# Four weight tiles at four different start addresses modulo 256, in a one-core decoder layer

## The chip, the cores and the metric

The kernel runs on one core of one Trainium2 chip. The metric is device time in microseconds of one launch. The kernel before takes 2124.78 us, the median of three runs that lie between 2121.08 and 2126.06 us.

## The reference

One decoder layer on 2048 tokens of width 1024, all in float32: gated linear attention (GLA) with 4 heads, then a gated feed-forward network with a short causal convolution, each followed by a residual and a layer norm, and each with a shift, a scale and a gate computed from a conditioning vector. Cut to what matters here:

```python
def gla_mixer(h, w_in, w_a2, b_a, norm_g, w_o):
    q, k, v, r, a_lr = jnp.split(h @ w_in, ...)          # 1024 -> 3088 columns
    log_a = jax.nn.log_sigmoid(a_lr @ w_a2 + b_a) / 16
    ...                                                  # chunks of 64 tokens, state of 128 x 256 a head
    return (rms_norm(o) * norm_g * jax.nn.silu(r)) @ w_o

def conv_ffn(h, w_up, conv_w, conv_b, w_down):
    u, g = jnp.split(h @ w_up, 2, axis=-1)               # 1024 -> 2 * 2816 columns
    u = causal_conv3(u, conv_w) + conv_b
    return (jax.nn.silu(u) * g) @ w_down

x = layer_norm(alpha * x + (1 + gate) * sublayer(x * (1 + scale) + shift), g, b)   # twice
```

## The kernel before, in words

**Split products.** TensorE multiplies in the float32r format. To keep float32 precision each operand is split into a rounded part h and a remainder l. `split` (L103) makes h by a ScalarE copy (L104) and l by a VectorE subtraction (L107). `mm3` (L109) then issues three matmuls for a product: h by h (L110), h by l (L111), l by h (L112). Nearly all of TensorE's work is in these three lines. Each matmul loads a stationary operand of 128 columns (the profile's PEld rows) and streams a moving operand of 512 columns past it (the PE rows).

**Weights.** A split weight stands in a tile of the pool `hlp`: 128 partitions by 2 by 1024 elements of 4 bytes, 8192 bytes a partition, h in the first half and l in the second. `hl_tile` (L94) hands these tiles out under three tags: "h0" and "h1" with one buffer each and "h2" with two, so there are four tiles. In the profile all four are called hl. Every slice of them that a matmul reads starts a multiple of 512 bytes from the tile's start. A tile is filled in one of three ways: by `split` from a raw tile; by a DMA of the saved split weight (`hl<-wh_d`, 1 MB); or by a DMA of a raw weight into the second half, which is then split in place (`hl<-wf_d` and `hl<-wfc_d`, 512 KB, the output projection).

**Where things lie.** Pools are laid out one behind the other: small tiles (`const`, `smp`), the four raw tiles, the four hl tiles, the five temporaries of tag "t2", and so on. The hl tiles start at bytes 26112, 34304, 42496 and 50688 of each partition. All four are multiples of 256. So are the starts of the tiles that hold the other operand: xc (split activations of the input and feed-forward products), xg (split activations of the query and output projections), h (called h3 in the code: the narrow split weight of the feed-forward network) and dhl (both operands of the down product). The tile "still", which is multiplied by itself at the start to warm TensorE up, starts at 64 modulo 256. The two U tiles start at 0 and 128 modulo 256.

**Stages.** From 0 to about 500 us: the modulation vectors and the input projections (hl stationary with xc moving, and the other way round for the values). From about 500 to 860 us: the query projection of the second token block, the heads of the attention, the output projection (xg stationary with hl moving) and the first layer norm; TensorE alternates between short runs of split matmuls and plain float32 matmuls of the heads. From about 860 to 1690 us: the up product of the feed-forward network in a fixed loop of 44 rounds (h0, h1 and h2 tiles stationary, xc moving). To the end: the down product, whose operands are called dhl and every third time hl.

**What sets the order.** The order of the work is written out by hand (`at_unit`, `quarter`, `tick`), with priorities for some evictions. DMAs are issued on SyncE's queue.

Of the kernel before, what the change touches and what calls it, by code (L numbers as in the profile page):

```python
# [8 lines left out]
F32 = mybir.dt.float32  # L9
F32R = mybir.dt.float32r  # L10
# [6 lines left out]
P = 128  # L17
# [21 lines left out]
def kernel(  # L39
# [27 lines left out]
    smp = ctx.enter_context(tc.tile_pool(name="smp", bufs=6))  # L67
    rawp = ctx.enter_context(tc.tile_pool(name="rawp", bufs=4))
    hlp = ctx.enter_context(tc.tile_pool(name="hlp", bufs=4))
# [5 lines left out]
    def order(later, earlier):  # L75
        tc.add_manual_dep(later.ins, earlier.ins.name,
                          mybir.DependencyInfo(mybir.DependencyClass.NoSync, mybir.DependencyReason.DATA),
                          reason="issue order")
# [4 lines left out]
    def psum(tag, bufs=1):  # L83
        return ps.tile([P, 512], F32, tag=tag, name="ps_" + tag, bufs=bufs)
# [4 lines left out]
    def z_tile(name="z"):  # L89
        return zp.tile([P, 1024], F32, tag="z", name=name)  # L90

    turn = [0]

    def hl_tile(tag=None):  # L94
        if tag is None:
            if turn[0] < 6:
                tag = ("h0", "h1", "h2", "h2", "h2", "h2")[turn[0]]
            else:
                tag = (("h2", "h2", "h0", "h1") if turn[0] < 32 else ("h2", "h0", "h2", "h1"))[(turn[0] + 2 * (turn[0] >= 48)) % 4]
            turn[0] += 1  # L100
        return hlp.tile([P, 2, 1024], F32R, tag=tag, name="hl", bufs=2 if tag == "h2" else 1)

    def split(h, l, src, lsrc=None):  # L103
        accs["copy"] = nc.scalar.copy(h, src)  # L104
# [78 lines left out]
    def rsqrt_eps(o, i):  # L183
        nc.gpsimd.tensor_scalar(o, i, EPS, None, op0=ALU.add)
        nc.gpsimd.tensor_tensor(o, o, mhalf[:, 0:o.shape[1]], op=ALU.pow)
# [268 lines left out]
    if True:  # L454
# [877 lines left out]
        def state(H, s):  # L1332
            po, old, h = H["po", s], H["S"][s], H["h"]
            new = S32[:, h] if s == 3 else ab.tile([P, DV], F32, tag="St", name="St", bufs=6)
            with tc.high_priority(offset=150):
                if old is None:
                    nc.vector.tensor_copy(new, po)
                else:
                    nc.vector.scalar_tensor_tensor(new, old, H["el"][:, 1, s:s + 1], po, op0=ALU.mult, op1=ALU.add)
            H["S"].append(new)  # L1340

        def head_c(H, g):
            h, v, Q = H["h"], H["v"], H["Q"]
            if g == 0:
                H["on"] = zp.tile([P, 4, DV], F32, tag="z", name="on")
                H["ss"] = smp.tile([P, 4], F32, tag="ss", name="ss")
            on = H["on"]
            po = psum("w", 4)
            at = H["at"][g]
            for i in range(2):  # L1350
                s = 2 * g + i
                pos_ = po[:, i * DV:i * DV + DV]
                st = H["S"][s]
                nc.tensor.matmul(pos_, at[:, i], v[s], start=True, stop=st is None)  # L1354
                if st is not None:
                    nc.tensor.matmul(pos_, Q[:, s, 0:128], st, start=False, stop=True)  # L1356
            if g == 0 and ("po", 3) in H:
                state(H, 3)
            with tc.high_priority(offset=150):
                nc.scalar.copy(on[:, 2 * g:2 * g + 2].rearrange("p s c -> p (s c)"), po)  # L1360
# [23 lines left out]
                store(g_d[H["tb"]][H["h"]].rearrange("p (s c) -> p s c", s=2), sr)  # L1384

        def normalise(z, after=None):
            st = smp.tile([P, 2, 6], F32, tag="bst", name="bst")
            for i in range(2):
                bn = nc.vector.bn_stats(st[:, i], z[:, i * 512:i * 512 + 512])
                if after is not None:  # L1390
                    order(bn, after)
            mv = smp.tile([P, 2], F32, tag="mv", name="mv")
            nc.vector.bn_aggr(mv, st)
            rs = smp.tile([P, 2], F32, tag="rs", name="rs")
            rsqrt_eps(rs[:, 0:1], mv[:, 1:2])
            nc.gpsimd.tensor_scalar(rs[:, 1:2], mv[:, 0:1], rs[:, 0:1], -1.0, op0=ALU.mult, op1=ALU.mult)
            nc.scalar.activation(z, z, AF.Identity, bias=rs[:, 1:2], scale=rs[:, 0:1])
# [184 lines left out]
        for m in range(16):  # L1582
            H = heads[m]
# [48 lines left out]
    if True:  # L1632
# [122 lines left out]
        for n in range(2 * NJ):  # L1755
# [5 lines left out]
            st = dict(j=j, hf=hf, W=W, X=X0 if hf == 0 else XN, refill=XN if n == NJ - 1 else None)  # L1761
# [130 lines left out]
    def ln2_last(p, b, t):  # L1892
        a, sm = acc.pop((p, b, t))
        st = sts.pop()
        nc.vector.bn_stats(st[:, 1], a[:, 512:1024])
        mv = smp.tile([P, 2], F32, tag="mv", name="mv")
        nc.vector.bn_aggr(mv, st)

        rs = smp.tile([P, 2], F32, tag="rs", name="rs")
        nc.scalar.activation(rs[:, 1:2], mv[:, 1:2], AF.Sqrt, bias=eps[:, 0:1])  # L1900
        ys = []
        for half in range(2):
            cs_ = slice(half * 512, half * 512 + 512)
            y = t2p.tile([P, 512], F32, tag="t2", name="y")
            i = nc.vector.scalar_tensor_tensor(y, a[:, cs_], mv[:, 0:1], rows[2][half], op0=ALU.subtract, op1=ALU.mult)
            if half == 0:
                order(nc.vector.reciprocal(rs[:, 0:1], rs[:, 1:2]), i)
            cut = (0, 256, 512) if t == 3 and half == 1 else (0, 512)
            for c0, c1 in zip(cut, cut[1:]):
                nc.vector.scalar_tensor_tensor(y[:, c0:c1], y[:, c0:c1], rs[:, 0:1], rows[3][half][:, c0:c1],  # L1910
                                               op0=ALU.mult, op1=ALU.add)
                store(outr[p * 8 + b * 4 + t][:, half * 512 + c0:half * 512 + c1], y[:, c0:c1])

    sts = []
# [29 lines left out]
    for p in range(2):  # L1944
        bank = {"A": [None] * 4, "C": [None] * 4}
        for i in ORDER:
            kind, b, half, whole = INTO[i]
            cs_ = slice(half * 512, half * 512 + 512)
            fresh = i in (0, 1, 4)
            ng = (NP + 1) // 2  # L1950
            outer = p == 1 and i == ORDER[-1]

            def mms(t, gi, got):
                n = min(2, NP - 2 * gi)
                h, w = got
                for k in range(n):
                    o = k * 512
                    mm3(bank[kind][t], (h[:, 0, o + t * P:o + t * P + P], h[:, 1, o + t * P:o + t * P + P]),
                        (w[:, 0, o:o + 512], w[:, 1, o:o + 512]),
                        fresh and gi == 0 and k == 0, gi == ng - 1 and k == n - 1, not fresh)  # L1960

            def evict(t):
                a, sm = acc[p, b, t]
                acc_out = {"accum_out": sm[:, half:half + 1]} if whole and not outer else {}
                nc.vector.scalar_tensor_tensor(a[:, cs_], bank[kind][t], 1.0, a[:, cs_],
                                               op0=ALU.mult, op1=ALU.add, **acc_out)
                if outer:
                    ln2_last(p, b, t)
                elif i in (3, 2):
                    work.append((ln2, p, b, t))  # L1970

            if fresh:
                bank[kind] = [psum("mm" if kind == "A" else "w", 4) for t in range(4)]
            if i == 3 and p == 0:
                work += [(init_acc, 1, 0, t) for t in range(4)]
            if outer:
                nc.vector.memset(eps, EPS)
                got = [d_get(q + gi) for gi in range(ng)]
                for t in range(4):
                    sts.append(smp.tile([P, 2, 6], F32, tag="bst", name="bst"))  # L1980
                    nc.vector.bn_stats(sts[-1][:, 0], acc[p, b, t][0][:, 0:512])
                    for gi in range(ng):
                        mms(t, gi, got[gi])
                        if gi % 3 == 1 and work:
                            f, *a_ = work.pop(0)
                            f(*a_)
                    evict(t)
            else:
                for gi in range(ng):
                    got = d_get(q + gi)  # L1990
                    if work and (gi > 0 or work[0][0] is init_acc):
                        f, *a_ = work.pop(0)
                        f(*a_)
                    for t in range(4):
                        mms(t, gi, got)
                        if gi == ng - 1:
                            evict(t)
            q += ng
        work += [(init_acc, 1, 1, t) for t in range(4)] if p == 0 else []
# [58 lines left out]
```

## Time and profile before

| What | Value |
|---|---|
| Median of three runs | 2124.78 us |
| The profiled execution | 2121.6 us |
| its span, first to last instruction | 2119.9 us |
| TensorE busy | 2085.8 us, 98% of the span, 9381 matmul records |
| VectorE, ScalarE, GpSimd busy | 1529.5, 1003.4, 107.0 us |
| DMA engines, mean busy share | 73.5% |
| granted TensorE clock, mean | 0.996 |

A plain float32 matmul leaves two records, a float32r one leaves one. A matmul's record is longer than its turn on the array: records overlap, since matmuls are pipelined. What a matmul costs is the distance from its start to the next one's start, which the timeline shows.

### The profile page before, as it was taken

To read this page: it belongs to the slowest core of one execution; us is meant where nothing else is said; L and a number is where in the kernel's file an instruction comes from. 1 tells how busy PE (TensorE), PEld (TensorE's weight loads), DVE (VectorE), ACT (ScalarE), POOL (GpSimd) and SP (SyncE) were. 2 spreads that over 40 slices of the span, in tenths; PEclk is the share of its full clock that TensorE was granted. 3 is DMA by queue.
4 is the path that set the end of the run, shared out by engine and by line. 5 is a ranking of instruction groups with operands and counts; after the bars stand their busy time and mean duration, and the time that the engine had idled before them with its cause. 6 is when DMAs were issued, how large, how long until landed. Compare 5 with 4: busy or idle time off the path is not lost.

```text
span 2119.9 us, 26188 instructions
## 1 busy us (share of the span) xinstructions
PE 2085.8 (98%) x9381; PEld 1721.9 (81%) x9381; DVE 1529.5 (72%) x2022; ACT 1003.4 (47%) x1405; POOL 107.0 (5%) x254
## 2 busy tenths in 40 slices
PE   9999999999999998999999999999999999999998
PEld 7887887778888787888888888888888888888886
DVE  6855757776687667878777787666676796577557
ACT  4648636674555544644444454333333443344332
POOL 0000000001112201100000000000000000020001
PEclk9999999999999999999999999999999999999999
DMA  9787888788745885777756679877777897677562
GB/s 336 304 295 261 283 306 286 268 306 317 277 145 196 310 289 192 274 249 285 273 194 219 219 253 321 288 258 273 246 276 256 295 325 250 206 247 251 189 200 89
DMA packets 192035, 546.24 MB, mean 258 GB/s; under 512 B 24928, under 2 KB 33504, under 8 KB 186272
## 3 DMA queue, kind: packets, MB, share of 16 engines
q1 hardware_dynamic: 191904, 544.56, 73.5%
q8 instruction: 74, 1.21, 0.2%
q14 instruction: 57, 0.47, 0.1%
HBM read 357.58 MB, written 186.91 MB: 257 GB/s over the span
## 4 chain that ended last, share of the span: by engine, by line
PE 71%; DVE 3%; ACT 2%; DMA 2%; issue 1%; POOL 1%; SPq 0%; DVEq 0%; POOLq 0%; ACTq 0%
PE ps_mm L110 15%; PE ps_mm L112 15%; PE ps_mm L111 15%; PE ps_w L111 7%; PE ps_w L110 7%; PE ps_w L112 7%; PE ps_w L1326 1%; PE ps_w L1354 1%; PE ps_w L1356 1%; PE ps_w L1310 1%; DMA hl<-wf_d 1%; DMA A<-a_d 0%; PE ps_w L1375 0%; PE ps_w L1416 0%; ACT on L1369 0%
## 5 line engine op out<-in xcount | busy, mean ns | idle before, releaser
L110 PE MATMUL ps_mm<-xc,hl 128*128 128x512 f32 x920 | 361.8, 393 | 6.2 <-ACT u L448 4.5
L111 PE MATMUL ps_mm<-xc,hl 128*128 128x512 f32 x920 | 359.5, 391 | 0.0
L112 PE MATMUL ps_mm<-xc,hl 128*128 128x512 f32 x920 | 358.8, 391 | 0.0
L110 PEld LDWEIGHTS ps_mm<-xc,hl 128*128 128x128 f32 x920 | 173.5, 189 | 46.4 <-ACT u L448 6.6
L112 PEld LDWEIGHTS ps_mm<-xc,hl 128*128 128x128 f32 x920 | 173.4, 189 | 36.5 <-DVE hl L107 0.2
L111 PEld LDWEIGHTS ps_mm<-xc,hl 128*128 128x128 f32 x920 | 173.6, 189 | 36.1 <-issue 0.5
L110 PE MATMUL ps_w<-xc,hl 128*128 128x512 f32 x464 | 180.6, 389 | 0.0
L111 PE MATMUL ps_w<-xc,hl 128*128 128x512 f32 x464 | 180.5, 389 | 0.0
L112 PE MATMUL ps_w<-xc,hl 128*128 128x512 f32 x464 | 180.5, 389 | 0.0
L1655 DVE SCALAR_TENSOR_TENSOR ct<-U,cw_sb,ct 128x512 f32<-128x512 f32 x176 | 131.8, 749 | 22.8 <-ACT ct L1649 20.2
L104 ACT CAST hl<-wu 128x1024 fp32r<-128x1024 f32 x90 | 94.8, 1053 | 104.1 <-PE ps_mm L112 76.9
L448 ACT COPY u<-ps_mm 128x512 f32<-128x512 f32 x112 | 65.3, 583 | 159.4 <-PE ps_mm L112 152.0
L104 ACT CAST dhl<-raw 128x1024 fp32r<-128x1024 f32 x57 | 60.1, 1054 | 159.2 <-PE ps_mm L112 98.5
L107 DVE TENSOR_TENSOR hl<-wu,hl 128x1024 fp32r<-128x1024 f32 x90 | 110.0, 1222 | 30.2 <-ACT hl L104 29.9
L107 DVE TENSOR_TENSOR dhl<-raw,dhl 128x1024 fp32r<-128x1024 f32 x57 | 69.7, 1223 | 65.4 <-ACT dhl L104 65.4
L107 DVE TENSOR_TENSOR hl<-raw,hl 128x1024 fp32r<-128x1024 f32 (+1 forms) x63 | 69.3, 1104 | 56.1 <-ACT hl L104 55.8
L110 PE MATMUL ps_mm<-hl,xg 128*128 128x512 f32 x240 | 104.0, 433 | 3.6 <-DVE z L1526 3.6
L104 ACT CAST hl<-raw 128x1024 fp32r<-128x1024 f32 (+1 forms) x63 | 60.0, 955 | 99.4 <-PE ps_mm L112 42.1
L104 ACT CAST hl<-wg 128x1024 fp32r<-128x1024 f32 x56 | 59.0, 1053 | 97.6 <-PE ps_mm L112 85.0
L110 PE MATMUL ps_mm<-dhl 128*128 128x512 f32 x264 | 102.7, 389 | 0.0
L111 PE MATMUL ps_mm<-dhl 128*128 128x512 f32 x264 | 102.7, 389 | 0.0
L112 PE MATMUL ps_mm<-dhl 128*128 128x512 f32 x264 | 102.7, 389 | 0.0
(284 smaller groups left out, 4743.7 us busy)
## 6 DMA issues: line engine op xcount, KB each, us to landing
hc_d<-ct SPq DMA_DIRECT2D x154, 256.0 KB, 2.9
raw<-hc_d SPq DMA_DIRECT2D x70, 512.0 KB, 4.2
draw<-wc_d SPq DMA_DIRECT2D x70, 512.0 KB, 4.6
wu<-in_wup_dram SPq DMA_DIRECT2D x44, 512.0 KB, 5.3
wg<-in_wup_dram SPq DMA_DIRECT2D x44, 512.0 KB, 4.3
wh_d<-hl SPq DMA_DIRECT2D x22, 1024.0 KB, 4.8
hl<-wh_d SPq DMA_DIRECT2D x22, 1024.0 KB, 6.6
mraw<-in_mws_dram SPq DMA_DIRECT2D x40, 512.0 KB, 6.0
```

The costliest lines, as they stand in the source:

```text
L104: accs["copy"] = nc.scalar.copy(h, src)
L107: return nc.vector.tensor_tensor(l, src if lsrc is None else lsrc, h.bitcast(F32), op=ALU.subtract)
L110: nc.tensor.matmul(po, a[0], b[0], start=first, stop=False, skip_group_check=resumed)
L111: nc.tensor.matmul(po, a[0], b[1], start=False, stop=False, skip_group_check=resumed)
L112: return nc.tensor.matmul(po, a[1], b[0], start=False, stop=last, skip_group_check=resumed)
L448: return t, nc.scalar.copy(t, po)
L1310: nc.tensor.matmul(pav[:, i], KI[:, s * P:s * P + P], Q[:, s], start=True, stop=True)
L1326: nc.tensor.matmul(pst[:, s % 2 * DV:s % 2 * DV + DV], KTt[:, s * P:s * P + P], v[s], start=True, stop=True)
L1354: nc.tensor.matmul(pos_, at[:, i], v[s], start=True, stop=st is None)
L1356: nc.tensor.matmul(pos_, Q[:, s, 0:128], st, start=False, stop=True)
L1655: nc.vector.scalar_tensor_tensor(ct, U[:, o + i:o + i + 512], cw_sb[:, j, i:i + 1], ct, op0=ALU.mult, op1=ALU.add)
```

## The change

Every hl tile becomes 2064 elements (8256 bytes) wide, of which the first 2048 are used, so that tiles that stand one behind the other start 64 bytes further modulo 256. The tag "h2" with two buffers becomes two tags, "h2" and "h3", that take turns, and each tag's tile gets its own name: hlp, hlq, hlr, hls. Room for the 256 bytes more comes from four kinds of small tiles of the pool `smp`, whose buffers go from 6 to 4 (ss, bst) or to 5 (mv, rs).

```diff
-    turn = [0]
+    turn, turn2 = [0], [0]
...
             turn[0] += 1
-        return hlp.tile([P, 2, 1024], F32R, tag=tag, name="hl", bufs=2 if tag == "h2" else 1)
+        if tag == "h2":
+            tag = ("h2", "h3")[turn2[0] % 2]
+            turn2[0] += 1
+        t = hlp.tile([P, 2064], F32R, tag=tag, name=dict(h0="hlp", h1="hlq", h2="hlr", h3="hls")[tag], bufs=1)
+        return t[:, 0:2048].rearrange("p (s c) -> p s c", s=2)
...
-                H["ss"] = smp.tile([P, 4], F32, tag="ss", name="ss")
+                H["ss"] = smp.tile([P, 4], F32, tag="ss", name="ss", bufs=4)
...
-            st = smp.tile([P, 2, 6], F32, tag="bst", name="bst")
+            st = smp.tile([P, 2, 6], F32, tag="bst", name="bst", bufs=4)
...
-            mv = smp.tile([P, 2], F32, tag="mv", name="mv")
+            mv = smp.tile([P, 2], F32, tag="mv", name="mv", bufs=5)
...
-            rs = smp.tile([P, 2], F32, tag="rs", name="rs")
+            rs = smp.tile([P, 2], F32, tag="rs", name="rs", bufs=5)
```

No instruction is added, removed or moved on any engine, and every wait is for the same semaphore and the same count as before. What differs is addresses. The hl tiles now start at bytes 25856 (hlp), 34112 (hlq), 42368 (hlr) and 50624 (hls): 0, 64, 128 and 192 modulo 256. The raw tiles move down by 256 bytes and stay multiples of 256; the tiles from "t2" on stay where they were.

The program's split matmuls with an hl tile as an operand, by the distance modulo 256 from the moving operand's start to the stationary operand's start:

| Distance | Matmuls before | Matmuls after |
|---|---|---|
| 0 | 6288 | 1776 |
| 64 | 0 | 2088 |
| 128 | 0 | 1128 |
| 192 | 0 | 1296 |

The other 2040 split matmuls of 512 columns and 128 stationary columns (dhl with dhl 1368, xc with h 672) keep a distance of 0.

More of the change, by code (lines that the diff above doesn't have):

```diff
@@ L1895, in ln2_last @@
         nc.vector.bn_stats(st[:, 1], a[:, 512:1024])
-        mv = smp.tile([P, 2], F32, tag="mv", name="mv")
+        mv = smp.tile([P, 2], F32, tag="mv", name="mv", bufs=5)
         nc.vector.bn_aggr(mv, st)
-        rs = smp.tile([P, 2], F32, tag="rs", name="rs")
+        rs = smp.tile([P, 2], F32, tag="rs", name="rs", bufs=5)
         nc.scalar.activation(rs[:, 1:2], mv[:, 1:2], AF.Sqrt, bias=eps[:, 0:1])
@@ L1979 @@
                 for t in range(4):
-                    sts.append(smp.tile([P, 2, 6], F32, tag="bst", name="bst"))
+                    sts.append(smp.tile([P, 2, 6], F32, tag="bst", name="bst", bufs=4))
                     nc.vector.bn_stats(sts[-1][:, 0], acc[p, b, t][0][:, 0:512])
```

## The prediction, made before the changed kernel ran

> **What bounds the kernel now.** I read the page's busy times first, then the stages, then the groups of matmuls, and last the timeline of single matmuls. The busy times and the chain:
>
> ```profile
> PE 2085.8 (98%) x9381; PEld 1721.9 (81%) x9381; DVE 1529.5 (72%) x2022; ACT 1003.4 (47%) x1405; POOL 107.0 (5%) x254
> PE 71%; DVE 3%; ACT 2%; DMA 2%; issue 1%; POOL 1%; SPq 0%; DVEq 0%; POOLq 0%; ACTq 0%
> ```
>
> TensorE bounds it, in every stage. The table by stage (us, then busy time of each engine with its instructions) has one stretch without any gap, the up product:
>
> ```profile
> 500.00:860.00 360.00, 345.61 (x1685) 289.71 (x1684) 263.94 (x419) 181.96 (x345) 50.69 (x115) 1.00 0.68 242
> 860.00:1660.00 800.00, 800.00 (x3543) 662.08 (x3542) 599.18 (x797) 332.30 (x449) 21.66 (x75) 1.00 0.74 260
> ```
>
> In the second row 3543 matmuls fill 800 us, 225.8 ns each. Only the pace of single matmuls can change this stage. The pace stands in the timeline of TensorE (start in us, length of the record):
>
> ```profile
> 1200.20 0.39 PE L110 MATMUL ps_mm<-xc,hl 128*128 128x512 f32 x1
> ...
> 1203.60 0.39 PE L110 MATMUL ps_w<-xc,hl 128*128 128x512 f32 x1
> ```
>
> There are 15 matmuls from the first start to the second: 3.40 / 15 = 226.7 ns. The down product has dhl for both operands, 12 matmuls between these two starts, and 2.72 / 12 = 226.7 ns again:
>
> ```profile
> 2030.06 0.39 PE L112 MATMUL ps_mm<-dhl 128*128 128x512 f32 x1
> ...
> 2032.78 0.39 PE L112 MATMUL ps_mm<-dhl 128*128 128x512 f32 x1
> ```
>
> The warm-up at the start multiplies "still" by itself with 256 moving columns. The first row is 17 such matmuls, and the second says when they were through:
>
> ```profile
> 6.87 2.20 PE L517 MATMUL ps_mm<-still 128*128 128x256 f32 x17
> 8.91 0.95 PE L544 MATMUL ps_w<-cs,mraw 128*128 128x1 f32 x8
> ```
>
> They take 2.04 / 17 = 120.0 ns each. Half the columns cost more than half the time: (226.7 - 120.0) / 256 = 0.417 ns a column, and 226.7 - 512 x 0.417 = 13.3 ns that does not depend on the columns. Plain float32 matmuls of 256 columns, two records each, pay nearly none of it. Here are 8 records in four rows, the next one two records after the last that is subtracted:
>
> ```profile
> 660.19 0.59 PE L1354 MATMUL ps_w<-v,attm 128*128 128x256 f32 x2
> 660.62 0.59 PE L1356 MATMUL ps_w<-St,Q 128*128 128x256 f32 x2
> 661.05 0.59 PE L1354 MATMUL ps_w<-v,attm 128*128 128x256 f32 x2
> 661.48 0.59 PE L1356 MATMUL ps_w<-St,Q 128*128 128x256 f32 x2
> ```
>
> From 660.19 to 661.48 are 6 records: 215 ns each, 11.7 ns less than a split matmul, and each loads the same 128 stationary columns. So each split matmul carries about 12 ns that another kind of matmul does not, while the next weights are loaded beside it. In the kernel before, both operands start at the same address modulo 256 in all these rows (0 for hl, xc, xg, dhl; 64 for "still"). No row shows a split matmul whose operands start at different ones. That is what the change makes, and all it makes.
>
> **The change part by part.** No instruction and no wait changes, so there are three terms: what TensorE's reads do, what ScalarE's and VectorE's accesses do, and what the DMAs do.
>
> TensorE's reads. Of the 6288 split matmuls with an hl operand, 4512 get operands at different addresses modulo 256 (2088 + 1128 + 1296 in the table of the change). The groups with the most of them:
>
> ```profile
> L110 PE MATMUL ps_mm<-xc,hl 128*128 128x512 f32 x920 | 361.8, 393 | 6.2 <-ACT u L448 4.5
> L110 PE MATMUL ps_w<-xc,hl 128*128 128x512 f32 x464 | 180.6, 389 | 0.0
> L110 PE MATMUL ps_mm<-hl,xg 128*128 128x512 f32 x240 | 104.0, 433 | 3.6 <-DVE z L1526 3.6
> ```
>
> The best end: the 11.7 ns are meetings of the two streams in the same part of the memory, and all of them go: 4512 x 11.7 = 53 us less. (With the 13.3 ns of the intercept it would be 60 us.) The bad end comes from the first matmuls after an interruption, which run slower than the steady pace with the same operands:
>
> ```profile
> 42.91 0.39 PE L110 MATMUL ps_mm<-xc,hl 128*128 128x512 f32 x1
> ...
> 44.99 0.39 PE L110 MATMUL ps_mm<-xc,hl 128*128 128x512 f32 x1
> 45.22 0.39 PE L111 MATMUL ps_mm<-xc,hl 128*128 128x512 f32 x1
> ...
> 46.35 0.39 PE L110 MATMUL ps_mm<-xc,hl 128*128 128x512 f32 x1
> ```
>
> Nine matmuls lie between 42.91 and 44.99: 2.08 / 9 = 231.1 ns. From 45.22 to 46.35 are five: 226 ns, the steady pace. In the output projection the runs are too short to get there:
>
> ```profile
> 659.03 0.40 PE L111 MATMUL ps_mm<-hl,xg 128*128 128x512 f32 x1
> ...
> 659.96 0.39 PE L112 MATMUL ps_mm<-hl,xg 128*128 128x512 f32 x1
> ```
>
> Four matmuls, 0.93 / 4 = 232.5 ns. So the extra time is not a constant of the instruction. It is something that settles, and it settled on a good value with equal addresses. If 4512 matmuls never settle, they cost 4512 x (231.1 - 226.7) = 20 us, or by the second pace 4512 x 5.8 = 26 us more. The term lies between -53 and +26 us.
>
> I take 0, because of the rates. The moving operand passes 4 bytes of each partition in 0.417 ns. The loading of weights is slower, by the warm-up of the modulation vectors, whose matmuls have a single moving column, so that loading is all they do:
>
> ```profile
> 46.58 0.95 PE L274 MATMUL ps_w<-ones,macc 128*128 128x1 f32 x8
> 47.39 0.48 PE L111 MATMUL ps_mm<-xc,hl 128*128 128x512 f32 x1
> ```
>
> Eight take 0.81 us, some 101 ns for 128 columns or 0.79 ns a column, about half the moving operand's speed. While 512 bytes of weights are read, the moving operand runs through some 970 bytes, and the distance between the two shifts by about 460 bytes, nearly two full rounds of 256. Whatever distance they start with, they pass through all distances about twice. A start 64, 128 or 192 bytes away changes when they meet and hardly how often. That is an argument from rates, not a measured row, so both ends stay in the range.
>
> The Trainium skill has a rule on this: "TensorE: Matmul & The Clock Gate", section "Step-by-step: what each phase is for", says that TensorE reads the two operands through two independent ports and that loading the next weights takes no read bandwidth from the running matmul. Its section "Wait — 56ns, not 53.3ns?" gives 215.7 ns from start to start for 512 columns at full clock. By the first the term is 0; by the second, a split matmul here is 11 ns too slow, and an estimate from the page's figure would be 4512 x 11.0 = 50 us less if unequal addresses restored it. The trace agrees with neither wholly: it has 226.7 ns beside loads, and the 215 ns only for the other format.
>
> ScalarE and VectorE. They write hl and read it back for the remainder. The tile view of U, whose two buffers start at 0 and 128 modulo 256 and are written 8 bytes further on, gives shortest, median and longest:
>
> ```profile
> L352 DVE TENSOR_TENSOR U<-ps_mm,p x44: 678/687/696, 855.5 to 1677.1; 128x512 f32<-128x512 f32 x44
> L1649 ACT ACTIVATE ct<-U,cb_sb,cw_sb x88: 807/815/820, 856.5 to 1696.5; 128x512 f32<-128x512 f32 x88
> ```
>
> Two starts, and all 44 or 88 within 18 ns: these engines do not see the phase. The term is 0, between -18 and +18 ns on an operation that TensorE's queue of ready tiles hides in any case; without that cover, the program's 274 splits into hl tiles, two steps each, at 18 ns would be 10 us.
>
> The DMAs. 30 loads of 512 KB and 22 of 1 MB go into hl tiles, and 22 of 1 MB come out. Only the loads of the output projection are waited for:
>
> ```profile
> ACT hl L104 <- DMA hl<-wf_d: 28.6, 12, 5.7
> hl<-wf_d SPq DMA_DIRECT2D x22, 512.0 KB, 4.6
> hl<-wfc_d SPq DMA_DIRECT2D x8, 512.0 KB, 3.5
> ```
>
> The first row is 28.6 us of waiting of ScalarE in 12 waits. The next two are loads of one size and one target, 1.1 us apart. I price the unknown effect between 0 and that spread taken as a share of the waits, 28.6 x 1.1 / 4.6 = 7 us, and take 0.5 us, near the lower end, since none of the bytes change. Behind ScalarE's wait stand its other copies, and TensorE waits for the split.
>
> Here a rule of the Trainium skill speaks against the change. "DMA: Bandwidth & Descriptors", section "How a descriptor splits into AXI transactions", says that a transaction must start at a multiple of 256 bytes, so that a piece that starts elsewhere costs an extra one. By it a row of 4096 bytes takes 17 instead of 16, and an estimate from that is 28.6 x 1/16 x 3/4 = 1.3 us more. No run here shows it yet.
>
> The smaller pools of ss, bst, mv and rs add no wait, so they cost nothing.
>
> Sum: 2121.6 us of the profiled execution + 0 + 0 + 0.5 = 2122.1. The median of the runs before is 3.2 us above the profiled execution; with it, 2125.3 us.
>
> **The rivals.** First, slower: the settled rhythm is lost. The rows at 42.91 and 659.03 speak for it: there is a good state and a worse one 4.4 to 5.8 ns away, and only equal addresses are known to reach the good one. The steady 226.7 ns in three stages with different tiles speaks against it, as does the fact that it is found again after every interruption. It decides as soon as the matmuls of hlq, hlr and hls average over 227.7 ns (4512 x 1.0 = 4.5 us, more than 0.2%). Its price is 20 to 26 us: 2145, up to 2151 and with the DMAs' bound 2158 us.
>
> Second, faster: unequal starts keep the streams apart. For it speaks that 215 ns exist with the same loads. Against it speak the rates, and that "still" pays the same 13.3 ns. In full it gives 2125 - 53 = 2072 us; if half of it goes, or if only two of the three distances are good, about 2098 us.
>
> Third, no change, my forecast: every hl matmul still at 226.7 ns whatever its name.
>
> **How the numbers follow.** A measurement of this kernel can tell about 0.2%, 4.2 us, from no change. No change has a chance of 0.45, slower 0.32, faster 0.23. Any real effect on 4512 matmuls of over 1 ns shows, so little lies between the cases. The likeliest gives 2125.3 us. Its own range is 2121 to 2132 (the spread of the runs below, the DMAs' 7 us above). The whole range goes up to 2158, which holds the slower case nearly all, and down to 2098, which holds half of the faster one: left out are about 0.12 below and 0.05 above.
>
> **What would show it right or wrong.** In the profile after, the four names make separate groups. Right: in the up product hlp, hlq, hlr and hls all start 226.7 ns apart, the stretch from 860 to 1660 us still holds about 3543 matmuls, and the median record stays 389 ns. The slower rival shows as records of 393 to 397 ns in the groups of hlq, hlr and hls and not of hlp; the faster one as a pace nearer 215 ns in those groups. A time that moves while all four paces stand still would show the DMA term mis-sized: longer waits for hlr or hls loaded from wf_d. The forecast is wrong if one address distance changes the pace by over 1 ns.

## The result: 0.84% slower, and the profile after

| What | Before | After |
|---|---|---|
| Median of three runs | 2124.78 us | 2142.70 us (2142.55 to 2143.16) |
| Profiled execution, its span | 2121.6, 2119.9 us | 2142.55, 2140.8 us |
| TensorE busy | 2085.8 us | 2110.7 us |
| TensorE idle in the span | 34.1 us | 30.1 us |

The ratio of the times is 1.0084, with a 95% interval of 1.0064 to 1.0105. The forecast was no change, 2125.3 us. What came is the slower rival, 2.3 us below the lower end of its price (2145). The time lies inside the whole range of 2098 to 2158 us, but outside the forecast's own range of 2121 to 2132. The busy times of the page after, and the shares of its chain of waits:

```profile
PE 2110.7 (99%) x9381; PEld 1724.3 (81%) x9381; DVE 1530.9 (72%) x2022; ACT 1001.3 (47%) x1405; POOL 106.0 (5%) x254
PE 87%; DMA 4%; ACT 4%; DVE 3%; issue 1%; POOL 1%; SPq 0%; DVEq 0%; ACTq 0%; POOLq 0%
```

TensorE still bounds the kernel, and the same 9381 matmuls keep it busy 24.9 us longer. VectorE and ScalarE are where they were (+1.4 and -2.1 us). The table by stage of the kernel after, in the columns of the one shown of before:

```profile
500.00:860.00 360.00, 347.77 (x1685) 290.97 (x1683) 260.81 (x415) 180.58 (x343) 50.01 (x115) 0.99 0.68 242
860.00:1660.00 800.00, 800.00 (x3481) 651.17 (x3480) 592.74 (x787) 328.12 (x445) 21.38 (x74) 1.00 0.73 256
```

In the stretch without any gap, 3481 matmuls fill the 800 us where 3543 did: 229.8 ns each instead of 225.8, at a granted clock of 1.00 both times. So the loss is in the pace of matmuls, not in a wait. The timeline of TensorE in the up product of the kernel after shows which ones. The rows left out are further matmuls of the same group, three for each product:

```profile
987.03 0.39 PE L114 MATMUL ps_mm<-xc,hlp 128*128 128x512 f32 x1
...
989.07 0.40 PE L114 MATMUL ps_mm<-xc,hlq 128*128 128x512 f32 x1
...
991.87 0.39 PE L114 MATMUL ps_mm<-xc,hlp 128*128 128x512 f32 x1
...
993.26 0.39 PE L114 MATMUL ps_mm<-xc,hlp 128*128 128x512 f32 x1
...
994.39 0.40 PE L116 MATMUL ps_mm<-xc,hlp 128*128 128x512 f32 x1
994.63 0.40 PE L114 MATMUL ps_mm<-xc,hlr 128*128 128x512 f32 x1
...
997.42 0.40 PE L114 MATMUL ps_w<-xc,hls 128*128 128x512 f32 x1
...
1000.23 0.39 PE L114 MATMUL ps_w<-xc,hlq 128*128 128x512 f32 x1
```

Nine hlp matmuls from 987.03 to 989.07 take 226.7 ns each, the pace of before. Then twelve hlq matmuls take 2.80 / 12 = 233.3 ns, twelve of hlr 2.79 / 12 = 232.5 ns, and twelve of hls 2.81 / 12 = 234.2 ns. The second group of hlp stands at distance 0 like the first, but comes behind hlq: its first six matmuls take 1.39 / 6 = 231.7 ns, the next five 1.13 / 5 = 226 ns. So unchanged matmuls pay too, for a moment, when they follow changed ones.

The distance alone doesn't tell a matmul's pace either. The twelve hls above, at distance 192, come behind hlr. A little later twelve hls come behind hlp, and take 2.75 / 12 = 229.2 ns:

```profile
1014.03 0.39 PE L114 MATMUL ps_mm<-xc,hls 128*128 128x512 f32 x1
...
1016.78 0.40 PE L114 MATMUL ps_w<-xc,hlr 128*128 128x512 f32 x1
```

In the whole trace, 23 runs of twelve hls behind hlp take 228.9 to 229.5 ns a matmul, and 24 runs behind hlr 233.2 to 233.8.

The lengths of the records show the loss more weakly. From the view by lines of the kernel after:

```profile
L114 PE MATMUL ps_mm<-xc,hlp 128*128 128x512 f32 x448 | 175.4, 392 | 0.0
L114 PE MATMUL ps_mm<-dhl 128*128 128x512 f32 x264 | 102.7, 389 | 0.0
L114 PE MATMUL ps_w<-xc,hlq 128*128 128x512 f32 x232 | 92.2, 397 | 0.0
L114 PE MATMUL ps_w<-xc,hls 128*128 128x512 f32 x112 | 44.5, 397 | 0.0
L114 PE MATMUL ps_w<-xc,hlr 128*128 128x512 f32 x112 | 44.4, 396 | 0.0
```

The three moved tiles have records of 396 and 397 ns, dhl has 389, and hlp lies between. But a part of this was there without the change: in the run with the four names and equal starts, told below, the same rows have 391 ns (hlp), 389 (dhl), 392 (hlq), 389 (hls) and 389 (hlr).

For the whole program I compared the start-to-start time of each float32r matmul of 512 columns with that of the same matmul before. Left out are the pairs with an interruption (over 260 ns in either trace):

| Distance after | Matmuls compared | ns before | ns after | us in all |
|---|---|---|---|---|
| 64 | 2027 | 227.1 | 233.1 | 12.3 |
| 128 | 1090 | 227.4 | 232.8 | 5.9 |
| 192 | 1254 | 227.3 | 230.6 | 4.2 |
| 0, hl and dhl | 3084 | 227.0 | 227.7 | 2.1 |
| 0, xc with h | 663 | 226.9 | 229.2 | 1.5 |

Together 26.0 us, against 24.9 us that TensorE is busier. The mean of 230.6 ns at distance 192 mixes the two paces of hls told above. The span grew by 4.0 us less than TensorE's busy time, since TensorE idles 30.1 instead of 34.1 us.

### The profile page after: what moved, and what is told of

It reads as the page before. It is cut to its first block, busy times and chain, and to the rows that moved or that the text cites. A ratio compares the mean times of both kernels' runs of the same rounds, so it can differ in the third digit from the quotient of the medians.

```text
span 2140.8 us, 26188 instructions
## 1 busy us (share of the span) xinstructions
PE 2110.7 (99%) x9381; PEld 1724.3 (81%) x9381; DVE 1530.9 (72%) x2022; ACT 1001.3 (47%) x1405; POOL 106.0 (5%) x254
## 4 chain that ended last, share of the span: by engine, by line
PE 87%; DMA 4%; ACT 4%; DVE 3%; issue 1%; POOL 1%; SPq 0%; DVEq 0%; ACTq 0%; POOLq 0%
PE ps_mm L114 18%; PE ps_mm L115 18%; PE ps_mm L116 18%; PE ps_w L114 9%; PE ps_w L115 8%; PE ps_w L116 8%; DMA mraw<-in_mws_dram 1%; PE ps_w L1358 1%; PE ps_w L1330 1%; PE ps_w L1360 1%; PE ps_w L1314 1%; DMA A<-a_d 1%; DMA hls<-wf_d 1%; PE ps_w L1379 1%; PE ps_w L797 0%
## 5 line engine op out<-in xcount | busy, mean ns | idle before, releaser
L114 PE MATMUL ps_mm<-xc,hlp 128*128 128x512 f32 x448 | 175.4, 392 | 0.0
L116 PE MATMUL ps_mm<-xc,hlp 128*128 128x512 f32 x448 | 175.1, 391 | 0.0
L115 PE MATMUL ps_mm<-xc,hlp 128*128 128x512 f32 x448 | 174.8, 390 | 0.0
L108 ACT CAST hlq<-wg 128x1024 fp32r<-128x1024 f32 x56 | 58.7, 1048 | 101.6 <-PE ps_mm L116 90.1
L356 DVE TENSOR_TENSOR u<-ps_w,u 128x512 f32<-128x512 f32 x60 | 41.2, 690 | 82.3 <-ACT u L452 77.9
L114 PEld LDWEIGHTS ps_mm<-xc,hlp 128*128 128x128 f32 x448 | 84.2, 188 | 18.5 <-issue 0.2
L115 PEld LDWEIGHTS ps_mm<-xc,hlp 128*128 128x128 f32 x448 | 84.1, 188 | 18.4 <-issue 0.2
L116 PEld LDWEIGHTS ps_mm<-xc,hlp 128*128 128x128 f32 x448 | 84.1, 188 | 17.9
L108 ACT CAST hlp<-wu 128x1024 fp32r<-128x1024 f32 x56 | 58.8, 1050 | 81.1 <-PE ps_mm L116 70.1
L1653 ACT ACTIVATE ct<-U,cb_sb,cw_sb 128x512 f32<-128x512 f32 x88 | 71.6, 814 | 50.5 <-DVE U L356 50.4
L115 PE MATMUL ps_w<-xc,hlq 128*128 128x512 f32 x232 | 92.2, 397 | 0.0
L114 PE MATMUL ps_w<-xc,hlq 128*128 128x512 f32 x232 | 92.2, 397 | 0.0
L114 PE MATMUL ps_mm<-xc,hlq 128*128 128x512 f32 x224 | 89.5, 400 | 2.7 <-ACT u L452 2.6
L116 PE MATMUL ps_w<-xc,hlq 128*128 128x512 f32 x232 | 92.2, 397 | 0.0
L114 PE MATMUL ps_mm<-xc,h 128*128 128x512 f32 x224 | 88.0, 393 | 1.0 <-ACT u L452 1.0
```

The lines of the kernel that those rows point to most:

```text
L114: nc.tensor.matmul(po, a[0], b[0], start=first, stop=False, skip_group_check=resumed)
L115: nc.tensor.matmul(po, a[0], b[1], start=False, stop=False, skip_group_check=resumed)
L116: return nc.tensor.matmul(po, a[1], b[0], start=False, stop=last, skip_group_check=resumed)
L356: return eng.tensor_tensor(o, a, b, op=op)
L1653: nc.scalar.activation(ct, U[:, o + 2:o + 514], AF.Identity, bias=cb_sb[:, j:j + 1], scale=cw_sb[:, j, 2:3])
```

## The experiments

The theory: the distance modulo 256 between the starts of the stationary and the moving operand sets the pace of a float32r matmul. The rivals: that the absolute address of the hl tiles, or of the DMAs' ends in the on-chip memory, costs; that more names, tags and smaller pools cost; or that any matmul behind one with other addresses is slow, whatever the distance. Each ratio below compares a run with runs of the kernel before that were taken beside it (medians of 2121.92 to 2123.03 us), with its 95% interval in brackets.

**The pace alone, by distance.** A kernel with nothing of the layer in it: groups of 120 matmuls of the split form, one behind the other, each group with operands of its own. It writes zeros, so its own time means nothing. The core of it, with one group for each distance:

```python
h, l = w[:, st:st + 128], w[:, st + 128:st + 256]                      # stationary, starts st bytes past a multiple of 256
xh, xl = x[:, mv:mv + cols], x[:, 512 + mv2:512 + mv2 + cols]          # moving
for n in range(40):
    for a, b, s, e in ((h, xh, first, False), (h, xl, False, False), (l, xh, False, last)):
        nc.tensor.matmul(po, a, b, start=s, stop=e)
```

> Nothing of the layer is computed: the kernel holds 25 groups of 120 split matmuls, each group with one pair of tiles, and writes zeros. Groups da to dp have the moving operand at 0 and the stationary one at 0, 16, 32 ... 240 modulo 256; ea and eb have both at 64 and both at 128; ec, ed, ee have the stationary operand at 0 and the moving one at 64, 128, 192; fa, fb, fc have the stationary one at 4, 8, 32. If the distance decides (theory A): 226.7 ns a matmul at distance 0 wherever both start (da, ea, eb), about 233 at 64 (de), 233 at 128 (di), 230 at 192 (dm), with ec like 192, ed like 128, ee like 64. If an operand off a multiple of 256 is slow by itself (B): ea and eb are slow as well, about 233. If only the switching between tiles with different starts costs (C): every group settles at 226.7. If DMAs or splits were the cause (D): 226.7 everywhere.

The timeline of TensorE folds 30 matmuls into a row. Group da has distance 0, db 16; de has 64, df 80; dm has 192, dn 208; ea has both operands at 64:

```profile
32.74 6.96 PE L65 MATMUL psa<-xda,wda 128*128 128x512 f32 x30
...
59.94 6.96 PE L65 MATMUL psa<-xdb,wdb 128*128 128x512 f32 x30
...
143.13 7.16 PE L65 MATMUL psa<-xde,wde 128*128 128x512 f32 x30
...
171.13 7.12 PE L65 MATMUL psa<-xdf,wdf 128*128 128x512 f32 x30
...
366.66 7.03 PE L65 MATMUL psa<-xdm,wdm 128*128 128x512 f32 x30
...
394.13 7.16 PE L65 MATMUL psa<-xdn,wdn 128*128 128x512 f32 x30
...
484.19 6.96 PE L65 MATMUL psb<-xea,wea 128*128 128x512 f32 x30
490.99 6.96 PE L65 MATMUL psc<-xea,wea 128*128 128x512 f32 x30
```

Distance 0: 27.20 / 120 = 226.7 ns. Distance 64: 28.00 / 120 = 233.3 ns. Distance 192: 27.47 / 120 = 228.9 ns. Both operands at 64: 6.80 / 30 = 226.7 ns. The others in the same way, each from its last 60 matmuls: 226.7 with both operands at 128; of the distances, 226.7 ns at 16 and 240; 229.8 at 176; 232.0 at 80; 234.3 at 96; 233.3 at 32, 48, 112, 128, 144, 160, 208 and 224; and even 4 and 8 bytes, behind such groups, 232.3 and 230.7. With the stationary operand at 0 and the moving one at 64 the pace is 228.9, at 128 it is 232.2 and at 192 it is 233.3 ns: within 1.2 ns of what 192, 128 and 64 give the other way round (228.9, 233.3, 233.3). So in this run the distance decides, its sign counts, and no distance is better than 0. At equal starts the absolute address does nothing.

**The change without its addresses.** The four names, the tags and the smaller pools stay, but a row is 2048 elements again, so all tiles start at 0:

```diff
-        t = hlp.tile([P, 2064], F32R, ...
+        t = hlp.tile([P, 2048], F32R, ...
```

> The changed kernel with rows of 2048 elements, so that all four named tiles start at 0 modulo 256 again; names, tags and the smaller small pools stay. A, B and C: 2125 us, no difference from before. If the smaller pools, the tags or the moved raw tiles were the cause (D): about 2142.

Measured: 2123.65 us, ratio to before 1.0002 [0.9991, 1.0012]. Names, tags, smaller pools and the moved raw tiles cost nothing that shows. The width of a row, and with it the starts of the hl tiles, is all that this run and the changed kernel differ in.

**All four tiles at one wrong distance.** Rows of 2048, a 64-byte tile ahead of the pool of the hl tiles, and 192 bytes behind it:

```diff
+    ahead_ = gaq.tile([P, 16], F32, name="ahead")
+    behind_ = gap.tile([P, 48], F32, name="behind")
...
-        t = hlp.tile([P, 2064], F32R, ...
+        t = hlp.tile([P, 2048], F32R, ...
```

> All four hl tiles at 64 modulo 256, everything else at a multiple of 256: one distance (64, or 192 where hl moves), no difference between the tiles. A: 4896 matmuls with hl stationary at distance 64 cost 6 ns each, those with hl moving at 192 some 3 ns: about +30 us, 2150 to 2160. B: the same or more, 2155 to 2165. C (switching between tiles): 2125.

Measured: 2151.85 us, 1.0134 [1.0115, 1.0153]. Two rows of the timeline of its up product, with the 12 hlr matmuls from the first to the second:

```profile
994.67 0.40 PE L119 MATMUL ps_mm<-xc,hlr 128*128 128x512 f32 x1
...
997.47 0.40 PE L119 MATMUL ps_w<-xc,hls 128*128 128x512 f32 x1
```

2.80 / 12 = 233.3 ns. With four equal starts, and no tile unlike another, it is slower than the change itself. So it isn't the variety of addresses that costs. It is the distance to the other operand.

**All large tiles at 64.** The hl tiles, xc, xg, h, dhl, the raw tiles and the rest of the large ones all move by 64 bytes: every distance is 0 again, and every DMA into them starts off a multiple of 256.

```diff
-        t = hlp.tile([P, 2064], F32R, ...
+        t = hlp.tile([P, 2048], F32R, ...
...
+    shift = const.tile([P, 16], F32, name="shift")
...
-    eps = pad.tile([P, 56], F32, name="eps")
+    eps = pad.tile([P, 104], F32, name="eps")
```

> All tiles, of both operands and of every DMA, 64 bytes further: no large tile starts at a multiple of 256, but every pair of operands has distance 0 again. A: 2125 us. B: slower than e_all64, 2160 or more, since both operands are off. If the DMAs' start addresses matter (D): slower than before by 5 us or more with the pace of matmuls unchanged at 226.7.

Measured: 2123.0 us, 1.0004 [0.9992, 1.0016]. Its table by stage has the up product at the old pace, 3543 matmuls in 800 us, and its busy times leave VectorE and ScalarE where they were:

```profile
860.00:1660.00 800.00, 800.00 (x3543) 662.13 (x3542) 599.92 (x799) 333.17 (x450) 21.64 (x75) 1.00 0.75 260
```

```profile
PE 2089.5 (98%) x9381; PEld 1726.0 (81%) x9381; DVE 1529.8 (72%) x2022; ACT 1003.2 (47%) x1405; POOL 105.8 (5%) x254
```

The same tiles as in the run before stand at 64, but now the other operand does too, and the whole loss is gone. The rivals of absolute addresses, for TensorE, the DMAs and the other engines, fall with this run.

**The fine structure.** Other distances, a second moving operand or a remainder at another start than the first, fewer moving and fewer stationary columns. Nothing of the layer is computed here either. The groups are lines like these (moving start, stationary start, moving columns, start of the second moving part, stationary columns, start of the remainder):

```python
('aa', 0, 256, 512, 0, 128, 256),
('ea', 0, 0, 512, 64, 128, 64),
('fc', 0, 0, 384, 0, 128, 0),
('ga', 0, 0, 512, 0, 32, 0),
```

> Nothing of the layer is computed: 25 groups of 120 split matmuls and a warm-up, zeros are written. Theory A says that the distance modulo 256 between the stationary operand that is being loaded and the moving operand that streams decides, and that the settled pace of the good zone is 226.7 ns. aa (distance 256): 226.7. ab, ac (248, 252): 226.7 if the good zone is round and 16 wide on both sides, as its ends 240 and 16 were good; but 4 and 8 were not (232.3 and 230.7), so by the rival of whole 16-byte lines (L) every distance that is no multiple of 16 is slow: ab, ac, ad (12) 230 or more, as ae (20), af (24) and ag (216). ba to be (the second moving operand 16 to 240 further, one matmul in three at another distance): between 226.7 and the pace of that distance, 227 to 231; bf (256): 226.7. ca to cc (the remainder's weights at 64, 128, 192): the same, 228 to 231. ea, eb (weights of a matmul at its own moving operand's distance, but the load beside it at another): if the operand that is loaded beside the stream counts, slower than 226.7; if a matmul's own pair counts, 226.7. fa to fc (128, 256, 384 moving columns): 128 is bound by the load at some 110 ns, 256 gives 120.0, 384 gives 173.3 (a fixed 13.3 ns). ga to gc (32, 64, 96 stationary columns): 216.7, 220, 223 if the fixed part is taken by the weights' reads; 226.7 if it is a fixed cost of a start.

From its timeline, three of them, with the row that follows each:

```profile
476.04 7.08 PE L66 MATMUL psa<-xea,wea 128*128 128x512 f32 x30
...
503.77 7.09 PE L66 MATMUL psa<-xeb,web 128*128 128x512 f32 x30
...
592.48 5.36 PE L66 MATMUL psb<-xfc,wfc 128*128 128x384 f32 x30
597.68 5.36 PE L66 MATMUL psc<-xfc,wfc 128*128 128x384 f32 x30
...
608.09 7.11 PE L66 MATMUL psa<-xga,wga 128*32 128x512 f32 x30
...
635.88 7.07 PE L66 MATMUL psa<-xgb,wgb 128*64 128x512 f32 x30
```

Distance 256 has 226.7 ns, and so has a second moving part 256 bytes on, behind a group at 235.0: 256 bytes is a full period. In ea the starts (stationary with moving) are 0 with 0, 0 with 64 and 64 with 0 in turn, and the pace is 27.73 / 120 = 231.1 ns; a second moving part at 64 alone gives 232.0. A load of 32 stationary columns, a quarter of the bytes, has 27.79 / 120 = 231.6 ns at distance 0, more than 128 columns have; 64 and 96 columns have 230.0. None of the values expected for these three came. With 384 moving columns it is 5.20 / 30 = 173.3 ns, with 256 it is 120.0: each 128 columns take 53.3 ns, and 13.3 ns are fixed. At distance 64 the columns take the same 213.3 ns if their rate holds, and 20 ns are left over. Neither number follows from how many bytes are read. Close to equal starts the run fits neither expectation: 252 has 226.7 but 248 has 233.3, and 12, 20 and 24 have 230.0, 233.3 and 231.1. So the good zone is not simply 16 bytes wide, and whole steps of 16 bytes don't mark it.

**All four at 192.** As with 64, but the tile ahead has 192 bytes and the one behind has 64:

```diff
+    ahead_ = gaq.tile([P, 48], F32, name="ahead")
+    behind_ = gap.tile([P, 16], F32, name="behind")
```

> All four hl tiles at 192 modulo 256. A, with the paces of the sweep (192: 228.9, 64: 233.3, 0: 226.7): 4416 matmuls with hl stationary cost 2.2 ns more, 9.7 us; 1392 with hl moving have distance 64 and cost 6.7 ns more, 9.3 us; less some 4 us of TensorE's idle time that shrinks, as it did with all tiles at 64: about +15 us, 2138. B (an operand off a multiple of 256 is slow by itself): as all tiles at 64, 2152.

Measured: 2135.92 us, 1.0068 [1.0046, 1.0091]. The names in a row are the moving operand, then the stationary one. So the first pair of rows of the timeline is distance 0 - 192 = 64, from the values' projection; the second is distance 192, from the up product:

```profile
71.04 0.39 PE L119 MATMUL ps_mm<-hlr,xc 128*128 128x512 f32 x1
...
74.31 0.39 PE L121 MATMUL ps_mm<-hlr,xc 128*128 128x512 f32 x1
```

```profile
978.95 0.39 PE L119 MATMUL ps_w<-xc,hlq 128*128 128x512 f32 x1
...
981.70 0.40 PE L119 MATMUL ps_mm<-xc,h 128*128 128x512 f32 x1
```

The first takes 3.27 / 14 = 233.6 ns, the second 2.75 / 12 = 229.2 ns. The same tile is dear as the moving operand and cheaper as the stationary one, as the sweep has it for 64 and 192. Here a ps_w row at distance 192 has the lower pace, so the result tile alone isn't what slowed the hls behind hlr in the changed kernel.

**Is there a distance or a mix better than 0?** Twelve mixes drawn at random, in which the three matmuls of a product have different distances, and groups with all starts within 16 bytes of a multiple of 256. Nothing of the layer is computed.

```python
('ae', 0, 48, 512, 112, 128, 0),
('bf', 0, 16, 512, 16, 128, 0),
```

> Nothing of the layer is computed: 24 groups of 120 split matmuls with different starts for the rounded part, the remainder of the weights and the second moving operand, drawn at random in steps of 16 (aa to al) or within 16 of each other (ba to bl); zeros are written. If the starts only have to lie within 16 of each other: all of ba to bl at 226.7, and aa to al between 229 and 235. If the settled state needs one and the same distance in every matmul (S): ba, bd, bj and every group with mixed starts over 228. A pace under 226.7 anywhere would show a better arrangement than equal starts; none is expected.

The mixes take 228.9 to 237.7 ns (last 60 of each), none less than 226.7. Of the groups near 0, seven have 226.7 and five between 228.9 and 233.3 ns, so neither expectation holds for all twelve. The seven have both moving parts at a multiple of 256, whatever the two stationary starts within 16 bytes; each of the five has a moving part at 16 or 240. No arrangement here beats the kernel before.

**One slice at 240, in the layer.** The first tile's slice starts 16 bytes below a multiple of 256, the others at 0:

```diff
+    ahead_ = gaq.tile([P, 56], F32, name="ahead")
...
-        t = hlp.tile([P, 2064], F32R, ...
-        return t[:, 0:2048].rearrange("p (s c) -> p s c", s=2)
+        o = 4 if tag == "h0" else 0
+        t = hlp.tile([P, 2048 + 2 * o], F32R, ...
+        return t[:, o:o + 2048].rearrange("p (s c) -> p s c", s=2)
```

> One tile, hlp, starts at 240 modulo 256, the other three at 0, so 1776 matmuls of hlp have a distance of 240 or 16 and are mixed with others at 0. If the sweep's price of each distance holds (A): those two cost nothing, 2122 us, no difference. If any inequality of starts costs (U): some 1776 x 4 to 6 ns, 2129 to 2133 us.

Measured: 2125.0 us, 1.0008 [0.9996, 1.0019], no change that can be told. That is the number expected, but in part for another reason. The timeline has a surprise, where hlp is the moving operand and the distance is 16:

```profile
81.07 0.40 PE L119 MATMUL ps_w<-hlp,xc 128*128 128x512 f32 x1
...
86.20 0.40 PE L120 MATMUL ps_w<-hlp,xc 128*128 128x512 f32 x1
...
86.66 0.39 PE L119 MATMUL ps_w<-hlq,xc 128*128 128x512 f32 x1
...
88.47 0.39 PE L118 MATMUL ps_w<-hlq,xc 128*128 128x512 f32 x1
```

22 matmuls take 5.13 / 22 = 233.2 ns, and behind them eight of hlq at distance 0 take 1.81 / 8 = 226 ns. In the sweep, distance 16 took 226.7. "The distance alone" fails here. Compared one by one with the kernel before, as above for the change, 470 matmuls at distance 16 take 233.7 ns instead of 227.9, 2.7 us in all, which the interval hides; 1415 at distance 240 take 226.9.

**What came before, or the moving operand's own start?** The groups cb and cd are the same (moving 0, stationary 16), one behind a group of distance 0 and one behind a group of distance 64; so are cf and ch (moving 240, stationary 0).

```python
('ca', 0, 0, ...), ('cb', 0, 16, ...), ('cc', 0, 64, ...), ('cd', 0, 16, ...), ('ce', 0, 0, ...),
('cf', 240, 0, ...), ('cg', 0, 64, ...), ('ch', 240, 0, ...), ('ci', 0, 0, ...),
```

> This kernel computes nothing of the layer and writes zeros; its own time says nothing, only the starts of its matmuls do. Groups of 120 split-form matmuls of 512 columns follow one another without a pause: ca (moving start 0, stationary start 0), cb (0, 16), cc (0, 64), cd (0, 16), ce (0, 0), cf (240, 0), cg (0, 64), ch (240, 0), ci (0, 0), cj (16, 0), ck (0, 64), cl (16, 0); then ia to il, each behind eight matmuls of two columns. cb, cf and cd, ch are the same distance of 16 bytes, entered from the pace of 226.7 ns (cb, cf) and from that of 233.3 ns (cd, ch). Theory, that what the streams did before decides at a distance near the edge: cb and cf 226.7 ns, cd and ch 233.3 ns, and behind the interruptions ib and ic 233.3 ns, ia, ii, ij, ik, il 226.7 ns, ie and if 233.3 ns. Rival, that the moving operand's own start decides at this distance: cb and cd both 226.7 ns, cf and ch both 233.3 ns, ib 226.7 and ic 233.3 ns. Under either, ca, ce, ci 226.7 ns and cc, cg, ck 233.3 ns.

```profile
33.03 6.96 PE L68 MATMUL psa<-xca,wca 128*128 128x512 f32 x30
...
60.23 6.96 PE L68 MATMUL psa<-xcb,wcb 128*128 128x512 f32 x30
...
87.43 7.16 PE L68 MATMUL psa<-xcc,wcc 128*128 128x512 f32 x30
...
115.44 7.17 PE L68 MATMUL psa<-xcd,wcd 128*128 128x512 f32 x30
...
143.44 6.98 PE L68 MATMUL psa<-xce,wce 128*128 128x512 f32 x30
...
170.66 7.16 PE L68 MATMUL psa<-xcf,wcf 128*128 128x512 f32 x30
...
198.66 7.15 PE L68 MATMUL psa<-xcg,wcg 128*128 128x512 f32 x30
```

cb takes 27.20 / 120 = 226.7 ns and cd 28.00 / 120 = 233.3: the same operands, two paces, by what ran before. Yet cf, with the same distance of 16 and also behind a group at 226.7, takes 28.00 / 120 = 233.3, and ch 236.5. cj and cl (moving 16, stationary 0) both take 231.6, one behind a group at 226.7 and one behind a group at 233.3. So both theories of this run are half right: near the edge of the good zone what ran before counts, and so do the starts themselves. At distance 0 neither does: ca, ce and ci have 226.7 to 226.9 ns, behind a group at distance 64 (ce) and behind ch (ci) too. Nor does it at distance 64: cc, cg and ck have 233.2 to 233.4. Behind eight matmuls of two columns, the last 60 of a group take 226.7 ns in ia and ik (distance 0), 233.3 in ib (16) and ie (64), 236.7 in ic (moving 240, stationary 0), 232.5 in if (128) and 228.9 in ig (192). The groups ii (distance 240), ij (moving 16, stationary 0, so 240 too) and il (252), for which the first theory had 226.7, take 228.3, 231.6 and 233.3. After an interruption only equal starts found the good pace again.

## Why the prediction was wrong, step by step

The forecast, no change at 2125.3 us, and its reason failed. That 2142.70 us lies inside 2098 to 2158 is owed to the width of the range, which had been drawn to hold the slower rival too (a chance of 0.32), and not to the reason.

- **That only the pace of single matmuls can change the up product** was right. 3543 matmuls in 800 us became 3481, and came back to 3543 in the run with all large tiles at 64. By the prediction's own sign, a pace moved by over 1 ns through one distance, the forecast is wrong.
- **The term of TensorE's reads** is the step that failed: "I take 0, because of the rates". The argument was that the two streams pass through all distances about twice whatever the start. The sweep refutes it: the start alone moves the pace from 226.7 to 233.3 ns. The term that was put at 0 measured 22.4 us over the 4371 compared matmuls at new distances. The group with 32 stationary columns speaks against a sum of meetings along the way as well: a quarter of the bytes is loaded, and the pace rises to 231.6 ns. The trace of before had a warning: it held two paces for the same operands, and a sum over a fixed path has one.
- **Its upper bound** was 20 to 26 us, from matmuls that "never settle". The 4371 compared matmuls at new distances cost 12.3 + 5.9 + 4.2 = 22.4 us, 5.1 ns each, or 23 us for all 4512. The rows at 42.91 and 659.03 thus gave the right size. Whether those first matmuls are in the same condition as distance 64 or 192 puts a matmul in isn't shown; only the size agrees.
- **The rival's evidence against itself**, that the steady pace is found again after every interruption, holds for equal starts alone: behind the interruption ia is back at 226.7 ns, ie settles at 233.3.
- **Not in the prediction**: matmuls whose addresses didn't change pay 3.6 us behind changed ones, and TensorE idles 4.0 us less. By span less busy time, TensorE idles 30.3 us in the run with all four at 64, 33.2 with all four at 192, and 33.9 (names alone) and 36.0 us (all large tiles at 64) with equal starts. That operands have more time to arrive is my reading, and no run tests it.
- **ScalarE and VectorE at 0** was right: 1001.3 and 1530.9 us busy after, 1003.2 and 1529.8 with every large tile moved.
- **The DMAs at 0.5 us** can't be told from 0. ScalarE's waits for the loads that mattered, in the kernel after, and then in the one with the four names at 0:

```profile
ACT hlr L108 <- DMA hlr<-wf_d: 13.0, 4, 6.2
ACT hls L108 <- DMA hls<-wf_d: 7.7, 5, 2.5
ACT hlp L108 <- DMA hlp<-wf_d: 6.0, 2, 3.8
ACT hlq L108 <- DMA hlq<-wf_d: 4.8, 2, 3.6
```

```profile
ACT hlr L108 <- DMA hlr<-wf_d: 16.8, 5, 6.7
ACT hlp L108 <- DMA hlp<-wf_d: 9.8, 3, 5.1
ACT hls L108 <- DMA hls<-wf_d: 7.1, 5, 2.6
ACT hlq L108 <- DMA hlq<-wf_d: 6.3, 2, 3.6
```

  That is 31.5 us in 13 waits with three tiles off a multiple of 256, and 40.0 us in 15 with none off. The prediction's 28.6 us had left out 10.0 us of waits for the loads from wfc_d, which changes nothing here. With every large tile off, the whole kernel stands at 1.0004 [0.9992, 1.0016], so by that interval all misaligned starts together cost at most 0.0016 x 2123 = 3.4 us. The Trainium skill ("DMA: Bandwidth & Descriptors", "How a descriptor splits into AXI transactions") counts an extra transaction for such a start. No cost of one shows here, in a kernel that TensorE bounds.
- **The faster rival** falls: no distance, mix or shift in these runs takes 512 columns below 226.7 ns. The Trainium skill ("TensorE: Matmul & The Clock Gate", "Step-by-step: what each phase is for") has the two operands read through independent ports, the next load taking nothing from the running matmul. By that one would expect no distance to matter, and the sweep, 226.7 against 233.3 ns by the start alone, disagrees.
- **The signs named beforehand** came: longer records for hlq, hlr and hls (396 and 397 ns in the rows above), and a pace over 227.7 ns. The lengths are not a safe sign by themselves. hlp has 392 ns, hlq has 392 in the same row with equal starts, and with all four tiles at 192 the rows at 233.6 and at 229.2 ns both show 0.39 us. The distance between starts tells what the length of a record doesn't.

What stays open is the mechanism: why 256 bytes, why the sign counts, why the moving operand's own start counts close to distance 0, and what TensorE carries from one group to the next.

## What to carry to other kernels

Where float32r matmuls run one behind the other, start the stationary and the moving operand at the same address modulo 256; common starts of 0, 64 and 128 served alike here, and a padded row that shifts one pool alone can cost some 5 ns a matmul. Moving both together by 64 bytes cost nothing that shows, so such an offset is no reason to repack a layout. When a trace shows two paces for one instruction, don't argue one of them away by rates: measure the pace alone, from start to start, in a kernel of a few hundred matmuls.

## What the runs showed of the hardware

- A float32r matmul of 512 columns, with the next 128 x 128 load beside it, settles in the sweep at 226.7 ns at equal starts modulo 256, 228.9 at 192, and 233.3 at 64 and 128. Mixes lie between and above, up to 237.7.
- The fixed part is 13.3 ns at equal starts, the same at 256, 384 and 512 columns. 233.3 is 6.7 ns above the pace of equal starts, and 228.9 is 2.2 above it. At 192 the three matmuls of a product don't pay alike: in the sweep their starts lie 231.7, 226.0 and 229.0 ns apart in turn.
- 128 columns take 111.7 ns, not the 66.7 that the line through the others gives. My reading is that the load of the next weights sets the pace there: eight matmuls of two columns, ahead of ia, take 0.81 / 8 = 101 ns each.
- The pace can depend on what ran before: at distance 16, with the moving operand at 0, 226.7 or 233.3 ns for the same operands, and at distance 192, in runs of twelve in the changed kernel, 229.2 or 234.2 ns in the rows shown. At distance 0, with 512 moving and 128 stationary columns, every group of 120 came back to 226.7.
